# One more piece of the down weights split in every fourth expert of a float32 transformer kernel

## The chip, the cores and the metric

The program runs on one core of one Trainium2 chip. The metric is the device time of one execution in microseconds (us). The core has a matrix engine (TensorE, PE in the profile; PEld is its loading of the stationary operand), a vector engine (VectorE, DVE), a scalar engine (ScalarE, ACT), GpSimd (POOL), and a sync engine (SyncE, SP), whose queue issues nearly all weight transfers here.

## The reference

A first block (attention over a context and the tokens, a Fourier mixer, and a mixture of experts) is followed by a second one (two layers with four feed-forward networks, an indexed attention and a gated mixer). There are 256 tokens of width 1024, all in float32. The change is in the mixture of experts: 32 experts of width 512, two for each token.

```python
def expert_block(args):
    tok, wt, e = args
    xb = h_pad[tok]
    y = (jax.nn.silu(xb @ w_gate[e]) * (xb @ w_up[e])) @ w_down[e]
    return y * wt[:, None]
```

Each expert has three matrices of 2 MB: `w_gate` and `w_up` (1024 x 512) and `w_down` (512 x 1024).

## The kernel before

**Split products.** The matrix engine multiplies float32 numbers either as they are, or in a faster reduced form, fp32r. The kernel makes nearly all products of weights in the fast form, and gets the precision back by splitting: `high` (L98) copies a weight piece on ScalarE into fp32r (`wh`, L104), `low` (L108) subtracts that from the piece on VectorE (`wl`, L113), and the products with `wh` and with `wl` are summed in PSUM. A piece used as it is, "native", needs neither copy nor subtraction, and its products run as plain float32.

**Pieces.** `moe_pieces` (L1441) writes the order in which the weights come: for each expert e the two halves of `w_gate` (pieces 0 and 1), the two halves of `w_down` of expert e - 1 (pieces 4 and 5), and the two halves of `w_up` (2 and 3). Each is 1 MB and lands in one of six `raw` buffers; the load of a piece is issued when the piece six places before it is `finished` (L89), which is after its `low`, or, when native, after its products (`raw_done`). There are five places for split pieces (four `wh`/`wl` and one `whx`/`wlx`).

**One expert, one round.** The tokens of an expert come as 128 stationary columns, 64 with the high parts and 64 with the low ones, so one piece takes eight matmuls of 512 columns. The loop over e (L1585) is software-pipelined over three experts, and under `manual_schedule` TensorE, ScalarE and VectorE run their instructions in the order in which the loop writes them. In round e:

- TensorE: gate products of e, first half (`rows(e, 0, 0)`), four transposes (`turn(1)`) and two (`place`) for e - 1, gate products second half, `scatter(e - 2)`, the down products of e - 1 in two halves (`down(e - 1, 0)`, `down(e - 1, 1)`), the up products first half (`rows(e, 1, 0)`), two gather parts for the next four experts (L1478, `G,xh` and `G,xl`, only in rounds below 28), four transposes (`turn(0)`, `idf,gu`), the up products second half.
- ScalarE: `leave` (copy out of PSUM), SiLU, copies `wh` of every piece up to (e, 2), `grown` (`GT`), the high half of `act`, copy (e, 3), `leave`, copies (e + 1, 0) and (e + 1, 1), `yhigh` twice, copy (e, 4), the gathered rows.
- VectorE: subtraction of (e - 1, 4), `total(1)`, a product, the low half of `act` (L170), in rounds 4, 8, ..., 24 also `hot` (two comparisons `G`, L1465), subtractions of every piece up to (e, 2), then (e, 3) and (e + 1, 0), `ylow` twice (`yl`, L1543), (e + 1, 1), `total(0)`.

`cut(which, e, n)` (L1564) makes all copies (or subtractions) in the list `names` up to piece (e, n). `names` holds the pieces that aren't native, in the order of the stream. So a piece that stops being native is taken along by the next call behind its place:

```python
cut(0, e, 2)        # ScalarE, ahead of grown and act
...
cut(1, e, 2)        # VectorE, behind act and hot
if last:
    scatter(e - 2)
if new:
    leave(e, 0)
if old:
    down(e - 1, 0)
```

PSUM has four banks for all of this (`bank_w`); four more hold the sum over experts. `down` takes two of the four, and `ylow` is the last to read them.

Of the kernel before, what the change touches and what calls it, by code (L numbers as in the profile page):

```python
# [29 lines left out]
class Net:  # L30
# [1401 lines left out]
                            nc.vector.tensor_add(self.h[t][:, o], self.h[t][:, o], a)  # L1432


    NATIVE = ((0, 5), (1, 5), (2, 5), (3, 5))

    def native(self, e, n):

        return (e % 4, n) in self.NATIVE

# [301 lines left out]
```

## Time and profile before

| what | value |
|---|---|
| median of three runs | 1874.41 us (1873.1 to 1874.9) |
| the profiled execution: its time, its span | 1874.24 us, 1872.5 us |
| busy share of the span: PE, PEld, DVE, ACT | 97%, 77%, 71%, 61% |
| stretch of the experts | about 235 to 757 us |
| subtractions and copies of 1 MB pieces in it | 156 each |
| plain float32 instructions (L161, `raw,act`) | 256, 8 for each expert |

The span is that of the instructions; 1.7 us of the execution's time lie around it. Busy shares are averages over stages with different limits. Matmuls overlap one another in the profile (their ends are modelled), so a busy PE is not PE at its peak.

### The profile page before, as it was taken

To read this page: it belongs to the slowest core of one execution; us is meant where nothing else is said; L and a number is where in the kernel's file an instruction comes from. 1 tells how busy PE (TensorE), PEld (TensorE's weight loads), DVE (VectorE), ACT (ScalarE), POOL (GpSimd) and SP (SyncE) were. 2 spreads that over 40 slices of the span, in tenths; PEclk is the share of its full clock that TensorE was granted. 3 is DMA by queue.
4 is the path that set the end of the run, shared out by engine and by line. 5 is a ranking of instruction groups with operands and counts; after the bars stand their busy time and mean duration, and the time that the engine had idled before them with its cause. 6 is when DMAs were issued, how large, how long until landed. Compare 5 with 4: busy or idle time off the path is not lost.

```text
span 1872.5 us, 22794 instructions
## 1 busy us (share of the span) xinstructions
PE 1809.4 (97%) x8305; PEld 1443.0 (77%) x8305; DVE 1335.0 (71%) x2114; ACT 1149.1 (61%) x1912; POOL 40.1 (2%) x73
## 2 busy tenths in 40 slices
PE   5999799999999999899999999999999999999998
PEld 2776567777777776688888888887888888887886
DVE  6987699989899988745567765556555776675554
ACT  5555488888788887644575654456454665465443
POOL 1000000000000000000000000000000011000000
PEclk8999799999999999999999999999999999999999
DMA  9884299999999999556464356654655555665540
GB/s 324 280 278 161 78 359 390 375 391 381 372 379 394 389 389 388 192 182 202 161 222 163 118 197 202 202 180 158 202 193 190 173 177 181 222 217 194 174 169 23
DMA packets 189267, 450.50 MB, mean 241 GB/s; under 512 B 9904, under 2 KB 118840, under 8 KB 164576
## 3 DMA queue, kind: packets, MB, share of 16 engines
q1 hardware_dynamic: 185056, 437.25, 65.3%
q0 software_dynamic: 3808, 11.25, 2.1%
q8 instruction: 66, 1.08, 0.2%
q10 hardware_dynamic: 288, 0.52, 0.1%
q14 instruction: 49, 0.40, 0.1%
HBM read 447.91 MB, written 1.07 MB: 240 GB/s over the span
## 4 chain that ended last, share of the span: by engine, by line
PE 83%; ACT 3%; DVE 2%; issue 1%; DMA 1%; ACTq 0%; DVEq 0%; SPq 0%
PE bank_w L161 59%; PE bank_acc L161 20%; PE bank_w L1524 1%; PE bank_w L316 1%; ACT wh L169 1%; DMA raw<-w_gate 1%; PE bank_w L247 0%; ACT xh L250 0%; PE bank_w L719 0%; ACT L192 0%; DVE wl L113 0%; ACT wh L104 0%; ACT L309 0%; PE bank_w L1487 0%; PE bank_w L507 0%
## 5 line engine op out<-in xcount | busy, mean ns | idle before, releaser
L170 DVE TENSOR_TENSOR wl<-raw,wh 128x512 fp32r<-128x512 f32 (+3 forms) x814 | 522.9, 704 | 252.2 <-ACT wh L169 251.5
L169 ACT CAST wh<-raw 128x512 fp32r<-128x512 f32 (+3 forms) x814 | 461.1, 635 | 268.2 <-PE bank_w L161 204.3
L161 PE MATMUL bank_w<-wh,xh 128*128 128x512 f32 (+2 forms) x1056 | 406.4, 385 | 4.1 <-ACT xh L250 3.4
L161 PE MATMUL bank_w<-wh,xl 128*128 128x512 f32 (+2 forms) x1056 | 402.7, 382 | 0.9 <-DVE xl L251 0.9
L161 PE MATMUL bank_w<-wl,xh 128*128 128x512 f32 (+2 forms) x1056 | 402.5, 381 | 0.0
L113 DVE TENSOR_TENSOR wl<-raw,wh 128x2048 fp32r<-128x2048 f32 x124 | 280.5, 2283 | 0.0
L104 ACT CAST wh<-raw 128x2048 fp32r<-128x2048 f32 x124 | 235.9, 1904 | 7.2 <-DMA raw<-w_gate 5.0
L161 PEld LDWEIGHTS bank_w<-wh,xh 128*128 128x128 f32 x1056 | 199.2, 189 | 42.5 <-ACT xh L250 6.5
L161 PEld LDWEIGHTS bank_w<-wh,xl 128*128 128x128 f32 x1056 | 199.1, 189 | 37.5 <-DVE xl L251 2.2
L161 PEld LDWEIGHTS bank_w<-wl,xh 128*128 128x128 f32 x1056 | 199.1, 189 | 35.0 <-issue 0.2
L161 PE MATMUL bank_w<-wh,XG 128*128 128x512 f32 x388 | 169.8, 438 | 0.0
L161 PE MATMUL bank_w<-wl,XG 128*128 128x512 f32 x388 | 152.2, 392 | 0.0
L161 PE MATMUL bank_acc<-wh,th 128*128 128x512 f32 x352 | 144.2, 410 | 0.0
L161 PE MATMUL bank_acc<-wh,tl 128*128 128x512 f32 x352 | 138.0, 392 | 0.0
L161 PE MATMUL bank_acc<-wl,th 128*128 128x512 f32 x352 | 137.7, 391 | 0.0
L309 ACT ACTIVATE silu<-bank_w,rs 128x256 f32<-128x256 f32 x88 | 41.6, 474 | 153.9 <-PE bank_w L161 153.7
L311 DVE SCALAR_TENSOR_TENSOR hid<-bank_w,rs,silu 128x256 f32<-128x256 f32 x88 | 42.5, 484 | 117.5 <-ACT silu L309 114.3
L161 PE MATMUL bank_w<-raw,act 128*128 128x512 f32 x256 | 115.0, 592 | 0.0
L161 PEld LDWEIGHTS bank_w<-wl,XG 128*128 128x128 f32 x388 | 73.1, 189 | 19.8 <-DVE wlx L113 5.3
L161 PEld LDWEIGHTS bank_w<-wh,XG 128*128 128x128 f32 x388 | 73.0, 188 | 20.0 <-issue 7.4
L161 PEld LDWEIGHTS bank_w<-raw,act 128*128 128x128 f32 x256 | 48.4, 189 | 48.5 <-issue 46.0
L161 PEld LDWEIGHTS bank_acc<-wh,tl 128*128 128x128 f32 x352 | 66.1, 188 | 14.1
(416 smaller groups left out, 2618.3 us busy)
## 6 DMA issues: line engine op xcount, KB each, us to landing
raw<-ffn_w_in SPq DMA_DIRECT2D x176, 512.0 KB, 5.0
raw<-w_gate SPq DMA_DIRECT2D x64, 1024.0 KB, 9.0
raw<-w_up SPq DMA_DIRECT2D x64, 1024.0 KB, 7.5
raw<-w_down SPq DMA_DIRECT2D x64, 1024.0 KB, 7.5
raw<-ffn_w_out SPq DMA_DIRECT2D x44, 1024.0 KB, 5.0
raw<-w_ada SPq DMA_DIRECT2D x16, 1024.0 KB, 5.9
raw<-a_w_in SPq DMA_DIRECT2D x12, 1024.0 KB, 6.5
raw<-b_w_in SPq DMA_DIRECT2D x12, 1024.0 KB, 5.2
```

Of the source, the lines that this page charges most:

```text
L104: self.nc.scalar.copy(wh[:, :k], self.pieces[i][:, :k])
L113: self.nc.vector.tensor_sub(wl[:, :k], raw[:, :k], wh[:, :k].bitcast(F32))
L161: self.nc.tensor.matmul(*a, **k)
L169: self.nc.scalar.copy(h, src)
L170: self.nc.vector.tensor_sub(l, src, h.bitcast(F32))
L309: nc.scalar.activation(s, ps[:, :256], AF.Silu, scale=self.rs[t])
L311: nc.vector.scalar_tensor_tensor(hid[c, t], ps[:, 256:], self.rs[t], s, op0=OP.mult, op1=OP.mult)
L316: nc.tensor.transpose(ps[:, r, :], hid[c, t][:, P * r : P * r + P], self.idf)
L1524: nc.tensor.transpose(tu[which][:, o], gu[which][:, o], self.idf)
```

## The change

The list `NATIVE` names the pieces that are used unsplit, as (expert modulo 4, piece). The change takes (3, 5) out of it.

```diff
-    NATIVE = ((0, 5), (1, 5), (2, 5), (3, 5))
+    NATIVE = ((0, 5), (1, 5), (2, 5))
```

So piece 5 of the experts 3, 7, ..., 31 (eight pieces) is copied and subtracted like the others, and `down(e, 1)` of these experts multiplies with `wh` and `wl`. For the experts 3 to 27 `cut` makes both in round e + 1: the copy goes in front of the copy of (e + 1, 2), the subtraction in front of the subtraction of (e + 1, 2). Piece (31, 5) has no later piece in `names`; it is split by `take` (L141) itself, when `down(31, 1)` asks for it.

## Rows read from the trace of the kernel before

**Rows 1.** The page: busy time by engine (PE), and the chain that ended last.

```profile
PE 1809.4 (97%) x8305; PEld 1443.0 (77%) x8305; DVE 1335.0 (71%) x2114; ACT 1149.1 (61%) x1912; POOL 40.1 (2%) x73
...
PE 83%; ACT 3%; DVE 2%; issue 1%; DMA 1%; ACTq 0%; DVEq 0%; SPq 0%
```

**Rows 2.** Two stretches of the experts: busy time by engine, granted clock, DMA share, GB/s.

```profile
280.00:328.00 48.00, 48.00 (x220) 36.90 (x220) 43.49 (x36) 39.27 (x41) 0.00 (x0) 1.00 0.98 388
616.00:664.00 48.00, 48.00 (x218) 36.45 (x217) 43.52 (x36) 39.42 (x42) 0.00 (x0) 1.00 0.97 382
```

**Rows 3.** Waits from 300 to 720 us: us in total, times, longest.

```profile
DVE sum L1528 <- PE bank_w L1524: 15.6, 23, 0.9
DVE act L170 <- ACT act L169: 13.1, 26, 1.3
...
ACT wh L104 <- DMA raw<-w_gate: 4.2, 7, 1.9
...
PE bank_w L161 <- DVE yl L1543: 0.8, 1, 0.8
```

**Rows 4.** VectorE in round 16, in order: start, duration, [idle before].

```profile
486.67 0.42 DVE L170 TENSOR_TENSOR act<-sum,act 128x256 fp32r<-128x256 f32 x1 [0.47 <-ACT act L169]
487.01 1.28 DVE L1465 TENSOR_TENSOR G<-slots,posm 128x512 fp32r<-128x512 f32 x2
488.22 4.48 DVE L113 TENSOR_TENSOR wl<-raw,wh 128x2048 fp32r<-128x2048 f32 x2
492.62 2.28 DVE L113 TENSOR_TENSOR wlx<-raw,whx 128x2048 fp32r<-128x2048 f32 x1
494.82 1.40 DVE L1543 SCALAR_TENSOR_TENSOR yl<-bank_w,gslot,yh 128x512 fp32r<-128x512 f32 x2
```

**Rows 5.** ScalarE in round 16, in order.

```profile
483.58 1.90 ACT L104 CAST wh<-raw 128x2048 fp32r<-128x2048 f32 x1
485.37 0.37 ACT L1493 CAST GT<-bank_w 128x256 fp32r<-128x256 f32 x1
486.23 0.41 ACT L169 CAST act<-sum 128x256 fp32r<-128x256 f32 x1 [0.49 <-DVE sum L1598]
```

**Rows 6.** TensorE's weight loads in round 16, in order.

```profile
488.43 0.19 PEld L161 LDWEIGHTS bank_w<-wh,act 128*128 128x128 f32 x1
...
490.24 0.41 PEld L161 LDWEIGHTS bank_w<-raw,act 128*128 128x128 f32 x2
...
493.47 0.19 PEld L161 LDWEIGHTS bank_w<-wh,XG 128*128 128x128 f32 x1 [0.24 <-issue]
493.90 0.19 PEld L161 LDWEIGHTS bank_w<-wl,XG 128*128 128x128 f32 x1 [0.24 <-issue]
...
495.50 0.65 PEld L161 LDWEIGHTS bank_w<-G,xh 128*128 128x128 f32 x4
496.08 0.55 PEld L161 LDWEIGHTS bank_w<-G,xl 128*128 128x128 f32 x4
496.58 0.46 PEld L1524 LDWEIGHTS bank_w<-idf,gu 128*128 128x128 f32 x4
```

**Rows 7.** VectorE and TensorE in round 17, where a late piece held them up.

```profile
512.76 1.41 DVE L1543 SCALAR_TENSOR_TENSOR yl<-bank_w,gslot,yh 128x512 fp32r<-128x512 f32 x2 [1.78 <-ACT yh L1539]
...
513.57 0.74 PE L161 MATMUL bank_w<-G,xl 128*128 128x256 f32 x4 [0.80 <-DVE yl L1543]
...
514.23 0.65 PE L1524 MATMUL bank_w<-idf,gu 128*128 128x128 f32 x4
```

**Rows 8.** VectorE in round 14, which has no `hot`.

```profile
461.96 0.75 DVE L1543 SCALAR_TENSOR_TENSOR yl<-bank_w,gslot,yh 128x512 fp32r<-128x512 f32 x1 [0.45 <-ACT yh L1539]
```

**Rows 9.** Two places where the granted clock fell: columns as in rows 2.

```profile
756.10:759.50 3.40, 1.42 (x10) 1.03 (x10) 3.39 (x7) 1.37 (x3) 0.00 (x0) 1.00 1.03 402
759.50:762.90 3.40, 3.40 (x10) 2.63 (x9) 3.38 (x10) 2.02 (x7) 0.00 (x0) 0.51 0.94 317
...
1530.90:1534.40 3.50, 1.83 (x6) 0.76 (x6) 3.33 (x7) 3.46 (x8) 0.23 (x1) 0.99 0.09 36
1534.40:1537.80 3.40, 3.40 (x13) 3.40 (x12) 3.28 (x8) 2.56 (x6) 1.37 (x3) 0.50 0.56 155
```

## The prediction

> **What bounds the kernel now.** I read the page first: by its busy times and its chain TensorE sets the end [rows 1]. Then I cut the stretch of the experts into windows, because the change is only there. In both windows shown, 340 us apart, TensorE is busy for the whole 48.00 us at full clock, VectorE for 43.5 and ScalarE for 39.3, and the DMA engines move 382 to 388 GB/s at a share of 0.97 to 0.98 [rows 2]. So four resources are within a fifth of each other, and the sum of busy times decides nothing: what counts is who waits for whom. The waits of 420 us of this stretch say it [rows 3]. TensorE waits for another engine almost nowhere: one stall of 0.8 us, on `yl` of VectorE. VectorE's idle time has two shapes. It waits for TensorE's transposes (15.6 us in 23 waits), which is slack, and it waits in the middle of splitting `act` for ScalarE's half (13.1 us in 26), which is a round trip that comes back however late VectorE is. TensorE sets the pace, then, with VectorE close behind, and the question is how much room there is at the place where TensorE next depends on it.
>
> That place is the end of each round's `down`. The one stall shows it [rows 7]: the second gather part started at 513.57, when the first of two `yl` had ended, and the four transposes behind it at 514.23, just 0.06 us after the second ended (512.76 + 1.41 = 514.17). They need the two PSUM banks that `yl` reads last. In round 16 the second `yl` ended at 494.82 + 1.40 = 496.22 [rows 4] and the transposes started at 496.58 [rows 6]. **The room is 0.36 us**, less the 0.06 of the signal. Round 16 stands for rounds 4, 8, 12, 16, 20 and 24: these have the two `G` of `hot` on VectorE, 488.22 - 487.01 = 1.21 us, and are exactly the rounds into which the change puts a further subtraction. In a round without `hot` the second `yl` waits 0.45 us for ScalarE [rows 8], so there is room there; the change goes where there is none.
>
> **The change part by part.** *Matmuls.* Eight plain float32 instructions become eight fp32r ones. In the row the eight take 493.47 - 490.24 = 3.23 us, and the load behind them comes 0.43 us after its forerunner where 0.23 is usual; the eight fp32r ones ahead of them took 490.24 - 488.43 = 1.81 [rows 6]. TensorE has 3.23 + 0.20 - 1.81 = 1.62 us less to do in each of eight experts, 13.0 us in all. This is the whole gain, if nothing else binds.
>
> *The copy on ScalarE.* It stands in front of the copy of (e, 2), and so in front of `GT` and the high half of `act`. Copies follow each other at 485.37 - 483.58 = 1.79 us. `GT` then starts at 485.37 + 1.79 = 487.16 and the copy of `act`, at most 0.37 us later, at 487.5, against 486.23 before [rows 5]: 1.27 us late, since of the 1.79 only its 0.49 us of waiting is cover. The data are there: piece (15, 5) is loaded ahead of (16, 2) on the same queue, and the copy of (16, 2) started at 483.58 without a wait.
>
> *The subtraction on VectorE.* The low half of `act` slips by the same 1.27, to 487.94; `hot` follows to 489.49; and the new subtraction stands there in front of those of (e, 2), (e, 3) and (e + 1, 0), at (492.62 - 488.22) / 2 = 2.20 us each. `yl` comes 1.27 + 2.20 = 3.47 us late: its second half ends at 496.22 + 3.47 = 499.69, and the transposes can start at 499.75 instead of 496.58 [rows 4, 6]. **That is 3.17 us later than before**, and the 1.62 us that TensorE saved lie inside its waiting: `act` is ready at 487.94 + 0.42 = 488.36, just in time for 488.43; the second `down` half waits for its own subtraction, which ends at 489.49 + 2.28 = 491.77, about 1.3 us; the up products wait 0.4 us for that of (e, 2); they end at 495.6, where they ended before. What is late next is `total(0)`, behind the transposes by data, and `total(1)`, 3.2 us later by VectorE's own queue: both keep their distance to TensorE, so the following round is as before, and being paced by TensorE it gives nothing back. Six rounds: 6 x 3.17 = 19.0 us.
>
> *Round 28* has no `hot` and no gather. I take 3.17 - 1.21 = 2.0 us; its bounds are 0 (its room hides it) and 3.2 (a round like the others). Sum 21.0.
>
> *Piece (31, 5)* is split when `down(31, 1)` asks for it, behind `act`. A copy of 1.90 and a subtraction of 2.28 stand against the 1.81 us of the first `down` half, so TensorE can wait up to 2.4 us, and saves at best 1.6. I take 0 and keep both ends.
>
> *Loads.* The raw buffer of piece 5 is released by its subtraction at about 491.8 instead of after its products at 493.5, the next ones up to 3.5 us later than now, with a consumer that is 3.2 us later: cost 0. The waits of copies for transfers are short now (4.2 us in 7) [rows 3]; were this cover gone, one of them would cost 0.6 us on average.
>
> *The clock.* In each of six rounds TensorE has nothing to do from about 496.2, when `G,xh` is through, to 499.1, when the first `yl` ends. Where it had been idle for about half of a stretch before, the granted clock fell: 1.42 us of work in 3.40, then 0.51, and 1.83 in 3.50, then 0.50, each time for the next 3.4 us [rows 9]. These are its two levels, 2.4 and 1.2 GHz. A stretch of 3.4 us at half clock costs up to 1.7 us of work. The bounds are 0 and 1.7 for each round; I take 1.2, nearer the upper end because the pause here is as long as in the rows, and below it because part of the slow stretch can pass while TensorE waits anyway. 6 x 1.2 = 7.2 us.
>
> Sum: -13.0 hidden in the waits (not counted), +19.0 + 2.0 + 0 + 7.2 = +28.2 us on the profiled execution's 1874.24 us (span 1872.5 and 1.7 around it), which lies 0.2 us under the median of the runs. That gives **1902 us**, 1.5% more.
>
> **The rivals.** *TensorE sets the pace after all* (faster). Its 13.0 us come through, less nothing: 1874.2 - 13.0 = 1861 us. For it: TensorE is busy in all of 48 us, and VectorE, with 2.28 us more in four rounds, would still be busy for less time than TensorE. Against it: the room of 0.36 us where 3.47 would have to be hidden. It decides the matter if the gather and the transposes don't have to wait for `yl`, or if ScalarE and VectorE reach the new work earlier than their order says. Chance 0.10. The Trainium skill (Perfetto Trace Analysis, Identifying the Most-Contended Engine) says to improve the engine with the highest occupancy, and to judge TensorE by its weight loads, not by its matmuls. By matmuls that rule gives this rival, -13.0 us; by weight loads, 36.45 of 48 here, VectorE with 43.5 comes first, and the change loads that one. The trace bears out the second reading.
>
> *The two sides cancel* (same). VectorE's lateness takes just what TensorE saves. This needs the delay at the transposes to be 0 to 0.6 us, that is some 2.6 us of cover more than the rows show: 1871 to 1877 us. Chance 0.06.
>
> *Only the subtraction counts, or the clock holds* (slower, less). If the copy's 1.27 us are hidden, each round costs 1.9 us: 1874.2 + 6 x 1.9 + 0.7 = 1886 us; if only the clock holds, 1874.2 + 21.0 = 1895 us. Chance 0.22.
>
> *The delay spreads* (slower, more). If the clock falls in the wait of 1.3 us too, or transfers that are issued late hold up the copies of the next round, a round costs about 5.5 us: 1874.2 + 33 + 3 = 1910 us. Chance 0.12.
>
> **How the numbers follow.** The forecast itself has 0.50: 1902 us, with a range of its own from 1895 to 1908. The range is to leave out 2 in 10: the two cases at 1861 and 1871 to 1877 (0.16), and the far ends of the slower ones. So 1880 to 1912. Within 0.2% (3.7 us) a measurement of this kernel can't tell a change from none. Faster 0.10, same 0.06, slower 0.84.
>
> **What would show it.** In round 16 of the changed kernel: the copy of `act` 1.3 us later behind `GT` and no longer waiting for VectorE; three subtractions between `G` and `whx`'s; a wait of the second `down` half on `wl`; a wait of 2.9 us of TensorE's gather on `yl`, under that name, in the list of waits; the granted clock below 1.00 for some 3 us behind it; rounds 1 to 3 of each four as long as before. The prediction is wrong if TensorE's waits for `yl` stay near nothing, if a group of four rounds gets shorter than before, or if the copy of `act` keeps its time. It is wrong in size if the clock stays at 1.00.

## The result and the profile after

The changed kernel takes 1898.18 us (median of four runs, 1896.07 to 1903.08) against 1873.76 for the kernel before (four runs, the three of the table ahead of the prediction and one more): the ratio is 1.0138, with a 95% interval from 1.0118 to 1.0158. It is slower by 1.4%. The profiled execution took 1897.41 us with a span of 1895.7, 23.2 us more than the span before. The longer one of the four executions took, the lower its mean granted clock, from 0.987 at 1896.07 us to 0.983 at 1903.08; all that follows is read from one execution of each kernel.

On the page TensorE is busy for 0.8 us less than before [rows 1] in a span that is 23.2 us longer, VectorE for 16.0 and ScalarE for 12.7 us more. VectorE's share of the chain was 2% and is 5%:

```profile
PE 1808.6 (95%) x8305; PEld 1445.2 (76%) x8305; DVE 1351.0 (71%) x2122; ACT 1161.8 (61%) x1920; POOL 40.5 (2%) x73
...
PE 79%; DVE 5%; ACT 3%; issue 2%; ACTq 0%; DVEq 0%
```

The two windows of [rows 2], after (busy time by engine, granted clock, DMA share, GB/s): TensorE is no longer busy throughout, the clock is below 1.00, and the transfers have slowed down with the consumer.

```profile
280.00:328.00 48.00, 44.28 (x204) 35.15 (x204) 41.14 (x34) 36.72 (x39) 0.00 (x0) 0.96 0.93 354
616.00:664.00 48.00, 44.28 (x193) 33.71 (x192) 41.46 (x32) 38.14 (x39) 0.00 (x0) 0.96 0.94 354
```

The waits from 300 to 742 us (total, times, longest) answer to [rows 3]. The one stall of 0.8 us on `yl` has become 17.1 us in 7, up to 2.7 at a time; `act` waits for ScalarE up to 1.7 us instead of 1.3; the waits of copies for transfers have gone but for one of 0.4 us.

```profile
DVE act L170 <- ACT act L169: 19.6, 26, 1.7
...
PE bank_w L161 <- DVE yl L1543: 17.1, 7, 2.7
...
PE bank_w L161 <- DVE wl L113: 3.6, 4, 0.9
...
ACT whx L104 <- DMA raw<-w_up: 0.4, 1, 0.4
```

Round 16 of the changed kernel, in order (start, duration, [idle before and what ended it]). ScalarE, for [rows 5]: two copies stand ahead of `GT`, and the copy of `act` follows `GT` without a wait.

```profile
495.50 3.70 ACT L104 CAST wh<-raw 128x2048 fp32r<-128x2048 f32 x2
499.10 0.36 ACT L1493 CAST GT<-bank_w 128x256 fp32r<-128x256 f32 x1
499.36 0.41 ACT L169 CAST act<-sum 128x256 fp32r<-128x256 f32 x1
```

VectorE, for [rows 4]: it waits 1.69 us for that copy where it waited 0.47, so ScalarE's copy costs 1.22 us; behind `G` stand four subtractions (the last that of (e + 1, 0), whose place has become a plain `wl`) instead of three, and only then `yl`.

```profile
499.81 0.43 DVE L170 TENSOR_TENSOR act<-sum,act 128x256 fp32r<-128x256 f32 x1 [1.69 <-ACT act L169]
500.15 1.29 DVE L1465 TENSOR_TENSOR G<-slots,posm 128x512 fp32r<-128x512 f32 x2
501.36 8.89 DVE L113 TENSOR_TENSOR wl<-raw,wh 128x2048 fp32r<-128x2048 f32 x4
510.16 1.40 DVE L1543 SCALAR_TENSOR_TENSOR yl<-bank_w,gslot,yh 128x512 fp32r<-128x512 f32 x2
```

TensorE's weight loads, for [rows 6]: the second `down` half waits 1.32 us for its own subtraction, the up products 0.51 us for the next one, and the second gather part 2.89 us for `yl`; the transposes follow.

```profile
503.69 0.19 PEld L161 LDWEIGHTS bank_w<-wl,act 128*128 128x128 f32 x1 [1.32 <-DVE wl L113]
...
505.89 0.19 PEld L161 LDWEIGHTS bank_w<-wl,XG 128*128 128x128 f32 x1 [0.51 <-DVE wl L113]
...
507.41 0.66 PEld L161 LDWEIGHTS bank_w<-G,xh 128*128 128x128 f32 x4
510.96 0.54 PEld L161 LDWEIGHTS bank_w<-G,xl 128*128 128x128 f32 x4 [2.89 <-DVE yl L1543]
511.62 0.42 PEld L1524 LDWEIGHTS bank_w<-idf,gu 128*128 128x128 f32 x4
```

Three of the six pauses are followed by a fall of the granted clock to 0.5 for 3.4 us. One of them, as windows (columns as above):

```profile
298.40:301.80 3.40, 0.69 (x6) 0.48 (x5) 3.40 (x4) 1.19 (x2) 0.00 (x0) 1.00 1.02 354
301.80:305.20 3.40, 3.40 (x14) 2.91 (x13) 3.40 (x4) 0.59 (x1) 0.00 (x0) 0.50 0.98 383
```

**Where the 23 us come from.** In each round I took the start of the transposes `turn(0)` (the matmuls of L1524) in a kernel's trace less that in the trace of before, and subtracted this difference in round 0. The table shows the shift in us, for the changed kernel and for six of the experiments below.

```
round          4     5     8     9    12    13    16    17    20    21    24    25    28    29    31
after       3.08  4.54  7.54  7.64 10.64 12.31 15.32 14.27 17.26 17.28 20.34 22.00 20.80 23.56 23.60
spare_both  3.15  4.56  7.59  7.67 10.68 12.32 15.34 14.27 17.24 17.29 20.34 21.93 21.98 23.51 23.55
spare_copy  0.79  0.88  1.69  1.75  2.56  2.65  3.47  2.42  3.19  3.22  4.07  4.12  4.16  4.18  4.22
spare_sub   1.77  1.86  3.67  3.75  5.56  5.64  7.45  6.40  8.16  8.19 10.04 10.08 10.13 10.47 10.51
copy_early  1.78  3.31  5.48  6.51  8.31  8.37 10.52 10.43 12.17 12.17 14.38 15.35 13.71 15.69 15.69
both_early  0.83  0.92  1.79  3.32  4.18  5.78  6.64  7.16  7.96  9.57 10.47 12.10 10.50 11.54 11.55
fill_wait   2.98  3.02  6.03  6.10  9.12  9.21 12.22 11.15 14.12 14.15 17.21 17.26 16.05 18.85 19.42
```

In the changed kernel rounds 4, 8, 12, 16, 20 and 24 add 3.08, 3.00, 3.00, 3.01, 2.99 and 3.06 us, 18.1 in all. The rounds behind the three falls of the clock (5, 13 and 25) add 1.46, 1.67 and 1.66, 4.8 in all. Round 17 takes back 1.05: the stall of [rows 7] is gone. From round 25 to 29 1.56 us are added, in another way than in the six. In round 28, which has no gather, the transposes don't wait for `yl`, and TensorE's saving brings them 1.19 us earlier. Round 29 then takes 2.75 us, with a wait of its first products for `yl` and one of its `down` for `act`:

```profile
717.86 0.50 PE L161 MATMUL bank_w<-wh,XG 128*128 128x512 f32 x1 [0.88 <-DVE yl L1543]
...
725.55 0.50 PE L161 MATMUL bank_w<-wh,act 128*128 128x512 f32 x1 [1.14 <-DVE act L170]
```

With small remainders the sum of all these is the 23.6 us of round 31, and the end of the kernel is just as late (23.2 us more span, from a start that lay 0.38 us earlier).

### The profile page after: what moved, and what is told of

Read it like the earlier page. It is cut to its first block, busy times and chain, and to the rows that moved or that the text cites. A ratio compares the mean times of both kernels' runs of the same rounds, so it can differ in the third digit from the quotient of the medians.

```text
span 1895.7 us, 22838 instructions
## 1 busy us (share of the span) xinstructions
PE 1808.6 (95%) x8305; PEld 1445.2 (76%) x8305; DVE 1351.0 (71%) x2122; ACT 1161.8 (61%) x1920; POOL 40.5 (2%) x73
## 4 chain that ended last, share of the span: by engine, by line
PE 79%; DVE 5%; ACT 3%; issue 2%; ACTq 0%; DVEq 0%
PE bank_w L161 56%; PE bank_acc L161 19%; DVE wl L113 2%; PE bank_w L1524 1%; PE bank_w L316 1%; ACT wh L169 1%; DVE wlx L113 0%; DVE G L1465 0%; DVE wl L170 0%; ACT xh L250 0%; PE bank_w L247 0%; DVE yl L1543 0%; PE bank_w L719 0%; ACT L192 0%; ACT junk L177 0%
## 5 line engine op out<-in xcount | busy, mean ns | idle before, releaser
L113 DVE TENSOR_TENSOR wl<-raw,wh 128x2048 fp32r<-128x2048 f32 x130 | 294.0, 2283 | 0.0
L104 ACT CAST wh<-raw 128x2048 fp32r<-128x2048 f32 x130 | 245.6, 1908 | 0.4 <-DMA raw<-w_gate 0.4
L161 PE MATMUL bank_w<-wl,XG 128*128 128x512 f32 x400 | 158.4, 396 | 0.4
L161 PE MATMUL bank_w<-raw,act 128*128 128x512 f32 x192 | 86.3, 592 | 0.0
L113 DVE TENSOR_TENSOR wlx<-raw,whx 128x2048 fp32r<-128x2048 f32 x33 | 75.4, 2284 | 4.0 <-ACT whx L104 4.0
```

The costliest lines, as they stand in the source:

```text
L104: self.nc.scalar.copy(wh[:, :k], self.pieces[i][:, :k])
L113: self.nc.vector.tensor_sub(wl[:, :k], raw[:, :k], wh[:, :k].bitcast(F32))
L161: self.nc.tensor.matmul(*a, **k)
```

## The experiments

My theory: the copy and the subtraction delay `yl` in the order of VectorE's queue, and what TensorE saves lies inside its waiting. The rivals: the split costs through its products; VectorE's load costs, wherever the work stands; transfers bind. Ratios are to the kernel before (1871.4 to 1872.9 us in the sessions of the experiments), with 95% intervals.

**The two operations without their use.** In the kernel before, the copy and the subtraction are made in their new places for seven of the eight pieces (not (31, 5)), and nobody reads them. The buffers of piece 5 are released where they were before. In `spare_copy` and `spare_sub` only one of them is made.

```diff
+            def spare(e, which):
+                i = self.find(self.rawi, False)
+                if which == 0:
+                    self.spare = self.places(i)
+                    nc.scalar.copy(self.spare[0], self.pieces[i])
+                else:
+                    wh, wl = self.spare
+                    nc.vector.tensor_sub(wl, self.pieces[i], wh.bitcast(F32))
...
+                    if old and e % 4 == 0 and e < 32:
+                        spare(e - 1, 0)
                     cut(0, e, 2)
...
+                    if old and e % 4 == 0 and e < 32:
+                        spare(e - 1, 1)
                     cut(1, e, 2)
```

> The kernel before, with the copy and the subtraction of piece 5 of the experts 3, 7, ..., 27 made where the change makes them, but nobody reads them: the products stay plain float32. Theory (the two operations delay yl in VectorE's queue, and what TensorE saves lies inside its waiting): as slow as the changed kernel, 3.1 us in each of six rounds and up to 2 in round 28, with one to six falls of the clock at 1.5 us, 1893 to 1900 us. Rival (TensorE is the pace and the split's cost lies in the new products and their wait on wl): no slower than before, 1874 us. Rival (TensorE's saving of 1.62 us counts in full in the changed kernel and only hides a larger loss): 13 us above the changed kernel, about 1911 us.

Measured: 1899.59 us, ratio 1.0150 (1.0133 to 1.0168). That is the changed kernel's time, and the table shows it round by round, within 0.1 us in all rounds but 28, falls of the clock included. So the whole loss is that of the two operations, and the eight faster products give nothing back (in round 28 they are 1.18 us ahead, in round 29 no longer). With plain products TensorE waits for `yl` 16.0 us in 6, with fast ones 17.1 in 7:

```profile
PE bank_w L161 <- DVE yl L1543: 16.0, 6, 2.7
```

Both rivals of this run are out. Transfers aren't the cause either: from 300 to 742 us the copies of the changed kernel wait for them 0.4 us in all.

> As spare_both, but only the copy on ScalarE, no subtraction. Theory: the copy pushes the high half of act back by 1.27 us, VectorE's queue follows, and of this 0.3 is room at the transposes: 0.9 to 1.0 us in each of six rounds, nothing in round 28, no fall of the clock: 1879 to 1881 us. Rival (only VectorE's busy time counts): 1874 us.

Measured: 1877.9 us, ratio 1.0033 (1.0021 to 1.0046). Each of the six rounds adds 0.8 us, nothing else does (round 17 takes its 1.05 back here too), and no fall of the clock occurs in the stretch. That a ScalarE copy of which VectorE knows nothing makes the kernel slower rules out that only VectorE's busy time counts.

> As spare_both, but only the subtraction on VectorE (the raw piece minus itself, so that it needs no copy). Theory: yl 2.20 us later, 1.9 us in each of six rounds, 0 to 0.9 in round 28, perhaps a fall or two of the clock at 1.5: 1885 to 1889 us; with spare_copy's excess it adds up to that of spare_both less 0.3 us a round. Rival (the ScalarE copy ahead of act is the whole delay): 1874 us.

Measured: 1884.14 us, ratio 1.0066 (1.0049 to 1.0083). Each of the six rounds adds 1.8 us. Together the two give 0.81 + 1.81 = 2.62; both at once give 3.03. The difference of 0.4 is the room at the transposes, which each of them had to itself: [rows 4] and [rows 6] made it 0.36.

**The same work in other places.** `copy_early` makes the copy at the end of the round before.

```diff
                     cut(0, e, 3)
+                    cut(1, e - 1, 5)
                     cut(1, e, 2)
...
                         rows(e, 1, 1)
+                    cut(0, e, 5)
```

The first added line leaves the subtractions of all rounds up to 31 where they were; in round 32 it splits piece (31, 5) ahead of its use.

> The changed kernel with the copy of piece 5 moved to the end of the round before, where ScalarE waits 1.67 us for TensorE; the subtraction stays. Theory: the 1.27 us of the copy vanish, the 2.20 of the subtraction stay: 1.9 us in six rounds, about 0.7 in round 28, fewer falls of the clock: 1885 to 1890 us, 8 to 13 below the changed kernel. Rival (VectorE's load is the cause, wherever ScalarE's copy stands): as the changed kernel, 1898 us.

Measured: 1889.58 us, ratio 1.0093 (1.0077 to 1.0110). The six rounds add 1.8 to 2.2 us, the copy's part is gone, and the clock falls behind four of them. `both_early` instead has the subtraction in front of `total(1)`:

```diff
                         cut(1, e - 1, 4)
+                        cut(1, e - 1, 5)
```

> The changed kernel with the copy at the end of the round before and the subtraction in front of total(1), where VectorE waits 0.86 us for TensorE. Theory: total(1) and act come 1.34 us later, act just in time for the down products (it was 1.3 us early), yl is 1.34 us late, the transposes 1.0 us: six rounds of about 1.0, round 28 nothing, no or few falls of the clock: 1878 to 1884 us. Rival (it is VectorE's load in these rounds, not the place of the work): as copy_early, 1885 to 1890 us.

Measured: 1885.71 us, ratio 1.0073 (1.0056 to 1.0090), more than I expected. The mechanism held (0.8 to 0.9 us in each of six rounds), but the pause is still 2.2 us long, since TensorE now saves its 1.62 us ahead of it and waits them out; the clock falls behind five of the six, 1.5 to 1.6 us each. I had taken the delay for the length of the pause. The waits of TensorE in it:

```profile
PE bank_w L161 <- DVE yl L1543: 13.0, 6, 2.2
```

Round 28 shows the saving by itself: its transposes come 1.62 us earlier, just what the prediction worked out, and round 29 takes 1.04 of it back.

**Another quarter of the experts**, whose round has no `hot`:

```diff
-    NATIVE = ((0, 5), (1, 5), (2, 5))
+    NATIVE = ((0, 5), (2, 5), (3, 5))
```

> The same change for another quarter of the experts: piece (1, 5) instead of (3, 5), so the new work falls into the rounds 2, 6, ..., 30, which have no hot. Theory: there the chain to yl has 1.5 us of room instead of 0.36, so 3.47 us of new work cost 2.0 us, in eight rounds, and the pause is too short for most falls of the clock: about 1890 us (1886 to 1893). Rival (the extra load counts the same in every round): as the changed kernel, 1898 us. Rival (hot is the whole cause): 1861 us.

Measured: 1893.46 us, ratio 1.0111 (1.0090 to 1.0131), between the theory (at most 1893) and its first rival. Counted in the same way as above, rounds 6, 10, 14, 18, 22 and 26 add 1.8 to 2.2 us, as expected for more room. But their pauses are as long as the changed kernel's (2.7 us by TensorE's matmuls), for the reason just given, and the clock falls behind five of these six. The size of the delay depends on `hot`; the falls come without it too.

**Every operation in a wait.** `best1` joins the three: piece (1, 5), both operations early, and in its rounds `yl` ahead of the subtraction of (e + 1, 0). `both_early_yl` is the same for piece (3, 5).

```diff
+                    late = old and not self.native(e - 1, 5)
+                    if not late:
+                        cut(1, e + 1, 0)
                     if old:
                         self.raw_done()
                         for half in range(2):
                             yhigh(e - 1, half)
                             ylow(e - 1, half)
+                    if late:
+                        cut(1, e + 1, 0)
```

> Piece (1, 5) split (no hot in its round), copy at the end of the round before, subtraction in front of total(1), and in these rounds yl in front of the subtraction of (e + 1, 0). Theory: every new operation then lies in a wait that ended before TensorE's next need, and TensorE's 1.62 us of saving in eight rounds come through: 1861 to 1865 us, faster than the kernel before. Rival (the DMA engines or VectorE's sum of work bind as soon as TensorE doesn't): 1874 us or more.

Measured: 1877.77 us, ratio 1.0028 (1.0017 to 1.0038). My theory of this version fell. Five of the eight rounds of the change do get shorter, by 0.7 to 0.8 us, but the next one gives it back, and a little more (0.9 to 1.0). The trace of rounds 6 and 7 shows how (timelines, in order of time). VectorE:

```profile
332.53 1.41 DVE L1543 SCALAR_TENSOR_TENSOR yl<-bank_w,gslot,yh 128x512 fp32r<-128x512 f32 x2 [1.67 <-ACT yh L1539]
333.85 4.48 DVE L113 TENSOR_TENSOR wl<-raw,wh 128x2048 fp32r<-128x2048 f32 x2
338.25 0.68 DVE L1528 TENSOR_REDUCE sum<-bank_w 128x256 f32<-128x512 f32 x1
```

ScalarE's SiLU behind it:

```profile
338.97 0.42 ACT L1591 ACTIVATE sum<-sum 128x256 f32<-128x256 f32 x1 [1.79 <-DVE sum L1528]
```

TensorE's weight loads one round later:

```profile
343.21 0.19 PEld L161 LDWEIGHTS bank_w<-wh,act 128*128 128x128 f32 x1 [1.03 <-DVE act L170]
```

Moved ahead, `yl` waits 1.67 us for ScalarE's `yh`, which stands behind copies there. The two subtractions then push `total(0)` behind them, SiLU waits 1.79 us for it, and one round later `act` comes 1.03 us too late. So VectorE's queue had room for only a part of the 2.20 us.

> As best1, but for piece (3, 5), so in the rounds with hot. Theory: yl is in time, but hot's 1.21 us and the new 2.20 us come back one round later, when total(1) is 1 us too late for act: between no change and 3 us faster, 1871 to 1876 us. Rival (the place of yl alone was the cause): as best1, 1861 to 1865 us.

Measured: 1875.53 us, ratio 1.0014 (1.0004 to 1.0024), in the range expected in time, but not faster: rounds 4, 8, ..., 24 gain 0.8 us each and the next ones lose about as much (0.9 to 1.0 without the stall of round 17). Neither version beats the kernel before.

**The subtraction on GpSimd.** As `copy_early`, with the subtraction of the new pieces on GpSimd, for one, two and all four of four experts.

```diff
+        self.nc.gpsimd.tensor_sub(wl[:, :k], raw[:, :k], wh[:, :k].bitcast(F32))
```

> The changed kernel (piece (3, 5) split), with its copy at the end of the round before and its subtraction on GpSimd, which is idle in this stretch, instead of VectorE. Theory (VectorE's queue is the cause, and not the split): yl keeps its time, TensorE's 1.62 us in eight experts come through if GpSimd needs less than some 7 us for the subtraction and doesn't slow VectorE: 1859 to 1863 us, faster than the kernel before. Rival (transfers or the copies on ScalarE bind as soon as TensorE is faster): 1871 to 1876 us. Rival (GpSimd is too slow or slows VectorE): above 1876 us.

> As pool_sub, with pieces (1, 5) and (3, 5) split. Theory: twice the gain of pool_sub, 1846 to 1852 us, with transfers at about 400 GB/s, below the 420 to 430 they reach in parts of the stretch. Rival (transfers bind): little under pool_sub, 1857 to 1863 us.

> As pool_sub, with piece 5 of every expert split. Theory of TensorE alone: 32 x 1.62 = 52 us, 1821 us; but 6.3 MB in 14.8 us would be 425 GB/s, the most that any part of the stretch shows, so transfers and VectorE (14.5 of 14.8 us busy) bind first: 1835 to 1850 us. Rival (GpSimd's use slows VectorE): above 1850 us.

Measured: 1892.31 us, ratio 1.0109 (1.0093 to 1.0124); 1909.28, 1.0199 (1.0185 to 1.0213); 1955.84, 1.0446 (1.0430 to 1.0461). The more pieces, the slower: the rival that GpSimd slows VectorE. In `pool_sub`, round 16, GpSimd and then VectorE:

```profile
493.26 5.59 POOL L122 TENSOR_TENSOR wl<-raw,wh 128x2048 fp32r<-128x2048 f32 x1 [62.48 <-ACT wh L104]
```

```profile
495.23 0.69 DVE L1536 TENSOR_REDUCE sum<-bank_w 128x256 f32<-128x512 f32 x1 [0.85 <-PE bank_w L1532]
496.02 3.11 DVE L1613 TENSOR_TENSOR sum<-sum,sum 128x256 f32<-128x256 f32 x1
```

The product of 256 columns on VectorE, 0.42 us in the changed kernel, takes 3.11 us and ends at 499.13, just after GpSimd's subtraction ended at 498.85; it is so in seven of the eight rounds with such a subtraction. The reduction out of PSUM ahead of it, in the same stretch, keeps its 0.69 us. `act` waits for the product. So this experiment doesn't tell whether a subtraction that costs VectorE nothing would bring TensorE's saving through.

**The clock by itself.** The first gather part of these rounds is computed five times over, so that TensorE works through most of its pause.

```diff
-                for j in range(2):
+                for j in [0, 1] * (5 if part == 0 and g > 1 else 1):
```

> The changed kernel, with the first gather part of the rounds 4, 8, ..., 24 computed five times over into the same bank (its last time is what is used), so that TensorE has some 2.3 us of work in its pause of 2.7 us before the first yl. Theory (the delay of yl is one cost, the fall of the clock in this pause another): the transposes come 3.0 us later than before in each of these rounds as in the changed kernel, the granted clock stays at 1.00, and the 4.8 us of its three falls are gone: about 1893 us. Rival (the falls of the clock cost nothing beyond the pause): as the changed kernel, 1898 us, or slower by what the extra products add.

Measured: 1894.44 us, ratio 1.0117 (1.0100 to 1.0134), with 16 more matmuls in each of six rounds than the changed kernel; the profiled span is 3.0 us shorter than the changed kernel's (1892.7 against 1895.7). By the ratios alone the two can't be told apart, since their intervals overlap; the rounds tell them apart. In the same stretch as above the clock stays at 1.00:

```profile
298.40:301.80 3.40, 3.40 (x25) 3.08 (x23) 3.40 (x2) 1.94 (x2) 0.00 (x0) 1.00 1.01 376
301.80:305.20 3.40, 2.60 (x15) 2.16 (x15) 3.40 (x4) 1.17 (x2) 0.00 (x0) 1.00 1.01 354
```

Each of the six rounds adds 3.0 us and the rounds behind them nothing (but for the 1.05 that round 17 takes back): 18.9 us at round 29 instead of 23.6, 19.4 at round 31. The falls of the clock are a cost of their own, 4.2 to 4.7 us in this pair.

## Why the prediction was right

- *The gain*: its size was right (round 28 of `both_early`, 1.62 us), and that it hides in the waits too. `spare_both` shows it directly: taking the faster products away again changes the time of no round but 28, and that one only until 29.
- *The copy* was to cost 1.27 us; the wait of `act` grew by 1.22, and alone it costs 0.81 a round. *The subtraction* was to cost 2.20; alone it costs 1.81. *The room* of 0.36 us is 0.4 by the three spare kernels.
- *The sum of a round*, 3.17 us, measured 3.03 on average; six rounds 18.1 us instead of 19.0. The waits inside it were foreseen at 1.3, 0.4 and 2.9 us and are 1.32, 0.51 and 2.89.
- *Round 28*: 1.6 us instead of 2.0, but not in the way of the text, which took it for a shorter delay of the same kind: the transposes of round 28 came earlier, and the loss stands in round 29. That the number is near is luck. *Piece (31, 5)*: 0, as taken. *Loads*: the cost of 0 held, and I had left out a gain, the 1.05 us of the stall in round 17, which vanished with the waits for transfers ahead of it.
- *The clock* was the mis-sized term. I took 1.2 us for each of six rounds, 7.2 in all; it fell behind three of six, at 1.46 to 1.67 us, 4.8 in all. So a fall costs nearly the upper bound of 1.7, and it comes or doesn't; a part of it in every round, as the sum has it, was in no round. Three rounds behind the six were longer for it, where the text wanted all of them as long as before. The pause of 2.9 us was called as long as those of [rows 9]; these have 3.40 - 1.42 = 1.98 and 1.67 us without work. With the 1.05 us of the stall and the smaller delay (0.9 and 0.4), this is all but 0.2 us of the distance from the 28.2 us forecast to the 23.2 of the span.

That TensorE sets the pace, the rival of 0.10, fails where the text put its condition: the gather does wait for `yl`. The rule of the Trainium skill (Perfetto Trace Analysis, Identifying the Most-Contended Engine) names VectorE once TensorE is judged by its weight loads, and `spare_sub` agrees, with 1.81 us a round for 2.20 us more of VectorE's work; but `spare_copy`, which loads ScalarE alone, is slower too, and that no occupancy tells.

What stays open: why the clock fell behind three of six pauses of the same length (2.7 us by TensorE's matmuls), and whether the saving comes through if the subtraction costs VectorE nothing. Of the 1.62 us of round 28 in `both_early`, 0.6 were left after round 29; in the other kernels of the table, in `best1` and in `both_early_yl` the round behind took back all that a round of the change had gained.

## What to carry to other kernels

When several engines are close to full and run fixed orders, don't compare busy times; find the one place where the pace-setter next waits for the loaded engine, and set the room there (here 0.36 us) against all that the change puts ahead of it in the queues, that of a third engine included. Work saved on the pace-setter ahead of such a place only lengthens its pause. A pause of 2 to 3 us can cost another 1.5 us through the clock, and this cost can be told apart by filling the pause with work that nobody needs.

## What the runs showed of the hardware

- A GpSimd subtraction of two SBUF tensors (5.59 us) held up a VectorE product of two SBUF tensors until it had ended: 3.11 us instead of 0.42. The Trainium skill (GPSIMD Engine Reference, Architecture) says that GpSimd's SBUF ports are shared with VectorE; this trace agrees, and shows that VectorE's product waits until GpSimd's instruction has ended.
- The granted clock fell from 2.4 to 1.2 GHz for 3.4 us behind pauses of 2.2 to 2.7 us, but not behind each: 3 of 6 pauses in the changed kernel, 5 of 6 in `both_early`, whose pauses are shorter, and none of the 6 of `spare_sub`, which are 1.5 us long.
